# Requesting the first attention tables during the second d-projection, with four layer-norm gate tiles

## The chip, the cores and the metric

The kernel runs on one core of a Trainium2 chip. The metric is the device time of one execution in microseconds (us), taken as the median of several runs. The five engines of the core are named as in the profile: PE (matrix multiply; PEld is its weight load), DVE (vector), ACT (scalar functions), POOL (GpSimd) and SP, which here only issues DMA transfers. Each engine takes its own instructions strictly in the order in which the program lists them; engines wait for one another and for transfers through semaphores.

## The reference, cut to what matters

Two layers run over 1024 latent tokens and 256 context tokens of width 1024. The first (even) layer is attention of two kinds. The second (odd) layer is the one that the change touches: a convolution branch of 512 channels and a neighbourhood attention with eight heads of 64, whose outputs are gated and multiplied by one output matrix.

```python
def odd_mixer(...):
    cv, cgl, cg, dq, dk, dv, dg = split_cols(h_lat @ w_in, ODD_WIDTHS)
    ...
    oc = conformer_conv(cv, cgl, cg, dw_w, dw_b, ln_g, ln_b)
    ...
    def d_row(args):                       # one of 16 grid rows of 64 queries
        r, qr = args
        rs = jnp.clip(r - kh // 2, 0, rows - kh)
        ...                                # 8 rows of keys, with a column window of 16
        bias = rpb[:, dr_idx][:, :, dc_idx] + col_mask[None, None]
        ...
        return gqa_attend(qr[:, :, :, None, :], kk, vv, bias).reshape(bsz, GRID_W, D_W)
    ...
    y_lat = jnp.concatenate([oc, od * jax.nn.silu(dg)], axis=-1) @ w_out

def conformer_conv(val, glu_gate, silu_gate, dw_w, dw_b, ln_g, ln_b):
    u = val * jax.nn.sigmoid(glu_gate)
    u = lax.conv_general_dilated(u, dw_w.reshape(C_CONV, 1, C_WIDTH), ...) + dw_b
    u = jax.nn.silu(layer_norm(u, ln_g, ln_b))
    return u * jax.nn.silu(silu_gate)
```

All of it is in float32. The kernel keeps that accuracy with a high and a low part of each operand, and three matmuls where one would do (`mm3`: high by high, high by low, low by high).

## The kernel before

**How the order comes about.** The kernel is written in program order, with generators that hand the turn to one another, and a planner then lays out each engine's instructions: by priority (which is program order, moved by `later`), by what its own timeline says is ready, and by when a tile of a pool comes free. So a transfer that stands late in the program can be issued much earlier on SP, if its source is written and its tile is free. What the planner fixes is an order for each engine; at run time an engine that waits holds up all that stands behind it.

**Pools.** Tiles live in pools that are opened and closed like a stack in the on-chip memory. A tile of a pool opened later may lie where a tile of a closed pool lay; its first write then waits for the last use of the old tile.

**The stages around the change.** The odd layer runs so:

1. The pool `cv` (and `u0`, closed at `ux.close()`): the projections of the convolution branch; then `d_proj(0)`, the first of four d-projections. Beside them run the convolution's 31 taps on DVE, ACT and POOL, for four blocks of channels. Their sums go to the DRAM tensor `Uc`, and the branch's gates to `Gc`.
2. The pool `ln`: `d_proj(1)`. After each of its 31 steps `pump(1)` runs one step of `ln_steps`, the layer norm of the convolution's output, in two halves of 512 tokens (c = 0, 1).
3. The pool `d1` (`dpool`): the attention of the odd layer in 16 groups (`groups1`), each one head and one half of the grid's columns. `weave` mixes its steps with `d_proj(2)`, `d_proj(3)` and the output projection; what is woven in stands some way ahead in priority.

**A d-projection** (`d_proj(i)`) covers two heads. It loads the weights of queries and keys as eight 128 x 256 blocks (`load_w`, L329: raw tile wr in three buffers; L296 on ACT casts the high part wh, L299 on POOL subtracts the low part wl), does the queries for two chunks of 512 tokens, the keys for three chunks (the last, 256 context tokens, is the one whose operand is called hc), loads the eight blocks of values and gates, and does these. Eight buffers hold wh and wl, so a value block is cast only when the last matmul with the query and key block of the same buffer is through. Results go to the DRAM tensors `QD`, `KD`, `VD` and `GD`; the parts of queries, keys and values are called spq, spk and spv. The products go through PSUM banks of which the tag "pp" has two.

**The layer norm** (`ln_steps`): one load of 1 MB (uc, L1138), three sums on POOL (L1141 to L1143), a matmul with ones that gives the mean (mu, L1148), four subtractions (L1152) with squares, the inverse deviation (`rstd_steps`), and for each of four blocks a scaling (L1167), a tanh, an addition, a product with the tanh and a product with the gate tile gc (L1172), which has one buffer; its load (L1166) stands in the same loop, as does a store of 256 KB to `Oc` (L1173).

**The start of attention.** `attn_gen` requests the tables of the first two groups (`next(p)`, which runs `load_q`: QH twice, QL, and the bias table bm of the row maxima, 540 KB); before that, `load_head(0)` loads the head's K (KAt, two transfers of 384 KB), and `copy_k` has ACT copy half of it to KBt (L564). The first group's `start` loads the bias tables bs of groups 0 and 1 (384 KB each), the second head's K and the V tiles. `k_tiles` and `v_tiles` have POOL set the constant parts of KBt and Vt (L355, L350). All of KAt, KBt, Vt, bm and bs lie in `d1`, which is opened when `ln` is closed.

Of the kernel before, what the change touches and what calls it, by code (L numbers as in the profile page):

```python
# [10 lines left out]
F32 = mybir.dt.float32  # L11
F32R = mybir.dt.float32r
ALU = mybir.AluOpType
# [5 lines left out]
P = 128  # L19
# [46 lines left out]
SQP = ((2, 3, 4, 5, 6), (), (4, 6))  # L66
ENDS = ((0, 0, 512), (1, 0, 256), (1, 256, 256))
LATE = 100
NFILL = (34, 34, 34)
HV = (('gggvvvvg',) * 3, ('gggvvvvg', 'vvvgvvvg', 'gggvvvvg'))  # L70
O1 = (6, 84, 46, 14)
# [16 lines left out]
def tile_kernel(ctx: ExitStack, tc: tile.TileContext, a, out):  # L88
# [22 lines left out]
    def nm(s):  # L111
        uid[0] += 1
        return f"{s}_{uid[0]}"
# [286 lines left out]
    def attn_gen(pool, groups, vshare, look, nexts=None):  # L400
# [30 lines left out]
                g.finish(g.ov, rb)  # L431

        for p in preps[:2]:
            next(p)
            yield
        for _ in range(2):
            yield
# [670 lines left out]
    with ExitStack():  # L1108
# [25 lines left out]
        def ln_steps(vp, c):  # L1134

            cs = slice(c * 512, (c + 1) * 512)
            uc = vp.tile([P, 4, 512], F32, tag="uc", name=nm("uc"), bufs=2)
            SY.dma_start(uc, Uc[:, :, cs])  # L1138
            s1 = vp.tile([P, 512], F32, tag="s1", name=nm("s1"), bufs=2)
            s2 = vp.tile([P, 512], F32, tag="s2", name=nm("s2"), bufs=1)  # L1140
            GP.tensor_tensor(s1, uc[:, 0], uc[:, 1], op=ALU.add)  # L1141
            GP.tensor_tensor(s2, uc[:, 2], uc[:, 3], op=ALU.add)
            GP.tensor_tensor(s1, s1, s2, op=ALU.add)  # L1143
            yield
            for _ in range(2):
                yield
            mu = bank("st", nm("mu"))
            PE.matmul(mu, ones5, s1, start=True, stop=True)  # L1148
# [12 lines left out]
            bc = yield from rstd_steps(vp, [s1], 512, "st", 2.0)  # L1161
            SC.copy(s2, bc)
            yield
            for i in range(4):
                gc = vp.tile([P, 512], F32, tag="gc", name=nm("gc"), bufs=1)
                SY.dma_start(gc, Gc[:, i, cs])  # L1166
                VE.scalar_tensor_tensor(uc[:, i], uc[:, i], lng[:, i : i + 1], s2, op0=ALU.mult, op1=ALU.mult)  # L1167
                th = vp.tile([P, 512], F32, tag="sql", name=nm("thl"), bufs=2)
                SC.activation(th, uc[:, i], AF.Tanh, scale=0.5, bias=lnbh[:, i : i + 1])
                VE.tensor_scalar(uc[:, i], uc[:, i], lnb[:, i : i + 1], None, op0=ALU.add)  # L1170
                VE.scalar_tensor_tensor(uc[:, i], th, 1.0, uc[:, i], op0=ALU.add, op1=ALU.mult)
                VE.scalar_tensor_tensor(uc[:, i], uc[:, i], 0.25, gc, op0=ALU.mult, op1=ALU.mult)  # L1172
                SY.dma_start(Oc[:, i, cs], uc[:, i])  # L1173
                yield

        def by_col(ap, c):
            return ap.rearrange("p (t r j) -> p r t j", t=5, j=8)[:, (c - 1) * 8 : c * 8]
# [5 lines left out]
        def d_proj(i):  # L1183
# [32 lines left out]
            for c in VORD:  # L1216
                t0, n = CHUNKS[c]
                pp = yield from proj1(wh, wl, 0, c)
                if c == 0:
                    vc = half("vc", "hf")  # L1220
                    SC.copy(vc[:, :n], pp[:, :n])
                    blocks = [(j, vc[:, j * P : (j + 1) * P]) for j in range(2)]
                    yield
                else:
                    for h_ in range(2):
                        SC.copy(by_col(vT[:, h_, :], c), window(pp, h_))
                    sg = half("sgd", "hf")
                    pp = yield from proj1(wh, wl, 1, c)
                    sgh = sg.rearrange("p (h r q) -> p h r q", h=2, q=32)
                    SC.activation(sgh, halves(pp), AF.Tanh, scale=0.5)  # L1230
                    for h_ in range(2):
                        VE.scalar_tensor_tensor(sgh[:, h_], sgh[:, h_], 1.0, halves(pp)[:, h_], op0=ALU.add, op1=ALU.mult)
                    SY.dma_start(GD[i][:, :, (c - 1) * 256 : c * 256], sg.rearrange("p (h q) -> p h q", h=2))
                    blocks = [(2 + 5 * h_ + t, vT[:, h_, t * P : (t + 1) * P]) for h_ in range(2)
                              for t in range(5 * (c - 1))]
                for k0 in range(0, len(blocks), 4):
                    bl = blocks[k0 : k0 + 4]
                    tr = bank(TRV, nm("trv"))
                    for k, (_, v) in enumerate(bl):
                        PE.transpose(tr[:, k * P : (k + 1) * P], v, ident)  # L1240
                    sp = pair("spv", 640)
                    n = len(bl) * P
                    sv = sp.rearrange("p a b -> p (a b)").rearrange("p (j s d) -> p j s d", s=2, d=64)
                    src = tr[:, :n].rearrange("p (j d) -> p j d", d=64)
                    split(src, sv[:, : 2 * len(bl), 1], sv[:, : 2 * len(bl), 0], "s", "v")
                    sv = sp.rearrange("p a b -> p (a b)").rearrange("p (j e d) -> p j e d", e=2, d=P)
                    k = 0
                    while k < len(bl):
                        e = k + 1
                        while e < len(bl) and bl[e][0] == bl[e - 1][0] + 1:  # L1250
                            e += 1
                        SY.dma_start(VD[i][:, bl[k][0] : bl[k][0] + e - k], sv[:, k:e].bitcast(F32))
                        k = e

        with tc.tile_pool(name="cv", bufs=1, reuse_waits="tile") as vp:
            stg[0] = vp
# [20 lines left out]
            for _ in bg:  # L1277
                pass
        ux.close()
        with tc.tile_pool(name="ln", bufs=1, reuse_waits="tile") as vp:  # L1280
            stg[0] = vp
            lnbh = vp.tile([P, 4], F32, tag="lnbh", name="lnbh")
            VE.tensor_scalar(lnbh, lnb, 0.5, None, op0=ALU.mult)
            ones5 = vp.tile([P, P], F32, tag="ones5", name="ones5")
            VE.memset(ones5, 1.0 / 512.0)

            def lns():
                for c in range(2):
                    yield from ln_steps(vp, c)
            bg = lns()  # L1290
            for _ in d_proj(1):
                pump(1)
            for _ in bg:
                pass

        dpool = ctx.enter_context(tc.tile_pool(name="d1", bufs=1, reuse_waits="tile"))
        stg[0] = dpool
        for _ in range(2):
            k_tiles(dpool, 12, 2)
        v_tiles(dpool, 7, 2)  # L1300
        od = [None, None]

        heads = {}
# [6 lines left out]
        def group1(gi, hd, hf):  # L1310
# [4 lines left out]
            def load_q(QH, QL):  # L1315
                SY.dma_start(QH[0:64, :].bitcast(F32), QD[i][ds, 0, hf])
                SY.dma_start(QH[64:128, :].bitcast(F32), QD[i][ds, 0, hf])
                SY.dma_start(QL[0:64, :].bitcast(F32), QD[i][ds, 1, hf])
                bm = dpool.tile([P, BMW], F32, tag="bm", name=nm("bm"), bufs=2)
                SY.dma_start(bm, a["d_bm"][hd, hf])  # L1320
                for b in range(4):
                    bms[b] = bm[:, BMO[b] : BMO[b] + (KROWS[b][1] - KROWS[b][0]) * NW]
# [335 lines left out]
```

## Time and profile before

| | us |
|---|---|
| median of 3 runs | 1566.41 |
| lowest and highest run | 1565.63, 1570.52 |
| profiled execution | 1564.79 |
| its span in the profile | 1563.0 |
| busy time of PE in the span | 1445.1 |
| busy time of DVE in the span | 1123.4 |

The profile is of one execution. The span is the time from its first to its last instruction; the device time of the same execution is 1.8 us longer. "Busy" counts instructions in execution. The views used below are: the page with its totals; windows, which give busy time, the clock granted to PE (1.00 is full speed), the share of the 16 DMA engines in use and GB/s in a stretch; the chain of waits, followed back from the last instruction; the timeline of one engine, with the idle time before an instruction and what ended it in square brackets; and the list of DMA issues with the median time from issue to landing. A line number such as L1172 is one of the kernel before. An engine name with a q (SPq) marks the instruction that issues a transfer, not the transfer.

### The profile page before, as it was taken

How to read it: one execution, taken by the hardware profiler on the slowest of the kernel's cores; microseconds unless marked ns; L12 is line 12 of the kernel's file. 1: busy time of each engine (PE TensorE's matmuls, PEld its weight loads, DVE VectorE, ACT ScalarE, POOL GpSimd, SP SyncE). 2: the span in 40 equal slices, each digit the busy share in tenths (PEclk: the TensorE clock that was granted, in tenths of full speed). 3: DMA queues.
4: the chain of work that ended last, by engine and by line, in shares of the span. 5: the costliest groups of instructions: out<-in, count | busy, mean ns of one | idle time of the engine just before them, and what ended most of it. 6: DMA issues, size and time to landing. Idle time of an engine off the chain costs nothing.

```text
span 1563.0 us, 22012 instructions
## 1 busy us (share of the span) xinstructions
PE 1445.1 (92%) x6984; PEld 1173.7 (75%) x6984; DVE 1123.4 (72%) x2172; ACT 753.6 (48%) x1545; POOL 825.5 (53%) x762
## 2 busy tenths in 40 slices
PE   6989989999999999899999889999998889999894
PEld 1878868887789678678887667888776678777784
DVE  4898897689858666654677667999655467676776
ACT  2731354445454755665455646444342355555472
POOL 1462464455555676776555656655442344255564
PEclk9899989999999999999999989999999899999997
DMA  9557345423441124731111122213545767797522
GB/s 340 190 163 240 89 123 167 148 67 118 145 137 44 53 90 144 225 110 38 41 44 41 61 95 61 74 63 128 172 158 186 241 198 214 218 271 219 167 73 108
DMA packets 181259, 213.66 MB, mean 137 GB/s; under 512 B 17164, under 2 KB 134616, under 8 KB 181144
## 3 DMA queue, kind: packets, MB, share of 16 engines
q1 hardware_dynamic: 174480, 200.69, 41.3%
q10 hardware_dynamic: 6664, 11.57, 2.3%
q8 instruction: 55, 0.90, 0.2%
q14 instruction: 60, 0.49, 0.1%
HBM read 152.17 MB, written 60.03 MB: 136 GB/s over the span
## 4 chain that ended last, share of the span: by engine, by line
PE 67%; DVE 14%; DMA 11%; issue 3%; POOL 2%; ACT 2%; SPq 1%; ACTq 0%; DVEq 0%; POOLq 0%
PE p L318 7%; PE p L320 7%; PE p L319 7%; PE ov L417 4%; PE ov L419 4%; PE ov L418 4%; PE po L320 4%; PE po L319 4%; PE po L318 4%; PE st L474 4%; PE st L478 4%; DVE macc L219 3%; DMA mw<-in_mod_w_dram 3%; PE pg L319 2%; PE pg L318 2%
## 5 line engine op out<-in xcount | busy, mean ns | idle before, releaser
L299 POOL TENSOR_TENSOR pl<-pf,ph 128x512 fp32r<-128x512 f32 (+3 forms) x321 | 391.2, 1230 | 260.7 <-ACT ph L296 211.3
L299 POOL TENSOR_TENSOR wl<-wr,wh 128x256 fp32r<-128x256 f32 (+2 forms) x256 | 197.1, 786 | 223.8 <-ACT wh L296 161.4
L486 ACT ACTIVATE pf<-st 128x512 f32<-128x512 f32 x284 | 166.1, 596 | 152.8 <-PE st L478 101.4
L296 ACT CAST ph<-pf 128x512 fp32r<-128x512 f32 (+3 forms) x364 | 205.6, 579 | 22.1 <-PE ov L418 12.4
L296 ACT CAST wh<-wr 128x256 fp32r<-128x256 f32 (+2 forms) x264 | 103.3, 404 | 184.0 <-DMA wr<-in_od_d_dram 40.7
L318 PE MATMUL p<-hh,wh 128*128 128x512 f32 x448 | 177.3, 399 | 6.4 <-ACT wh L296 4.2
L319 PE MATMUL p<-hl,wh 128*128 128x512 f32 x448 | 177.1, 397 | 0.2 <-POOL hl L299 0.2
L320 PE MATMUL p<-hh,wl 128*128 128x512 f32 x448 | 175.5, 401 | 0.1
L474 PE MATMUL st<-QH,KAt 128*128 128x512 f32 (+3 forms) x364 | 142.4, 393 | 14.1 <-ACT pf L486 12.1
L417 PE MATMUL ov<-ph,Vt 128*128 128x512 f32 (+3 forms) x364 | 140.6, 386 | 8.9 <-DVE y L640 6.4
L419 PE MATMUL ov<-pl,Vt 128*128 128x512 f32 (+3 forms) x364 | 140.6, 387 | 4.0 <-DVE pl L299 2.4
L478 PE MATMUL st<-QL,KBt 68*128 68x512 f32 (+3 forms) x364 | 137.7, 387 | 0.5 <-DVE QL L388 0.3
L418 PE MATMUL ov<-ph,Vt 128*64 128x512 f32 (+3 forms) x364 | 137.7, 378 | 0.0
L1125 DVE SCALAR_TENSOR_TENSOR cps<-U,taps,cps 128x512 f32<-128x512 f32 x184 | 124.2, 749 | 0.0
L219 DVE SCALAR_TENSOR_TENSOR macc<-mw,csil,macc 128x512 f32<-128x512 f32 x107 | 99.3, 949 | 16.4 <-DMA mw<-in_mod_w_dram 15.4
L598 DVE TENSOR_REDUCE mp<-mx 128x1 f32<-128x512 f32 x128 | 85.6, 682 | 34.6 <-PE mx L597 33.8
L318 PEld LDWEIGHTS p<-hh,wh 128*128 128x128 f32 x448 | 84.8, 189 | 26.4 <-ACT wh L296 4.8
L319 PEld LDWEIGHTS p<-hl,wh 128*128 128x128 f32 x448 | 84.9, 190 | 20.2 <-POOL hl L299 0.6
L320 PEld LDWEIGHTS p<-hh,wl 128*128 128x128 f32 x448 | 84.3, 189 | 20.3 <-POOL wl L299 0.5
L474 PEld LDWEIGHTS st<-QH,KAt 128*128 128x128 f32 x364 | 70.1, 193 | 34.4 <-ACT pf L486 19.9
L419 PEld LDWEIGHTS ov<-pl,Vt 128*128 128x128 f32 x364 | 70.1, 193 | 27.9 <-POOL pl L299 5.2
L417 PEld LDWEIGHTS ov<-ph,Vt 128*128 128x128 f32 x364 | 70.3, 193 | 24.5 <-issue 7.5
(277 smaller groups left out, 3530.1 us busy)
## 6 DMA issues: line engine op xcount, KB each, us to landing
mw<-in_mod_w_dram SPq DMA_DIRECT2D x34, 512.0 KB, 5.7
Q<-qs SPq DMA_DIRECT2D x40, 256.0 KB, 2.7
QH<-Q SPq DMA_DIRECT2D x80, 128.0 KB, 2.7
bm<-in_d_bm_dram SPq DMA_DIRECT2D x16, 540.0 KB, 6.2
wr<-in_od_d_dram SPq DMA_DIRECT2D x64, 128.0 KB, 2.7
mw<-in_mod_w_dram SPq DMA_DIRECT2D x28, 256.0 KB, 3.0
wr<-in_ev_qkv_dram SPq DMA_DIRECT2D x32, 192.0 KB, 2.9
KAt<-KD SPq DMA_DIRECT2D x16, 384.0 KB, 6.8
```

The costliest lines, as they stand in the source:

```text
L219: VE.scalar_tensor_tensor(t, w, csil[:, dk, q : q + 1], t, op0=ALU.mult, op1=ALU.add)
L296: SC.copy(hi, src)
L299: (GP if leng == "g" else VE).tensor_tensor(lo, src, hi.bitcast(F32), op=ALU.subtract)
L318: PE.matmul(o, lh, rh, start=first, stop=False)
L319: PE.matmul(o, lh, rl, start=False, stop=False)
L320: done[0] = PE.matmul(o, ll, rh, start=False, stop=last)
L417: PE.matmul(o, V[:, 64:192], ph, start=(t == 0), stop=False)
L418: PE.matmul(cut(g.ov[0:64], q0, n), V[:, 0:64], ph, start=False, stop=False)
L419: pvs.append(PE.matmul(o, V[:, 64:192], pl, start=False, stop=(last and g.sink is None)))
L474: sts.append(PE.matmul(sf, KA[:, cs], cut(g.QH, q0, n), start=True, stop=False))
L478: PE.matmul(sf, KB[0:68, cs], cut(g.QL[0:68], q0, n), start=False, stop=True)
L486: SC.activation(pf[:, :n], st[:, :n], AF.Exp, scale=1.0 if g.bias else SCALE)
```

## The change

It does the following:

- Opens a pool `t1` (`tpool`) ahead of `ln`, where the conv stage's tiles lay, and puts the K tiles (KAt, KBt, with POOL's memsets), bm and bs in it. Only V and the working tiles stay in `d1`, opened after layer norm as before.
- Requests the tables of the first two groups from the loop of `d_proj(1)`: after step 2 the tables of group 0, after 4 the first head's K, after 8 its copy on ACT, after 10 the tables of group 1, after 14 and 18 the bias tables bs of the two groups. `attn_gen` then skips its own request, and the first group's `start` loads no bs.
- Gives the layer norm's gate tile four buffers and issues the four loads of a half together, three steps after its uc load and ahead of the mean.
- Replaces the four stores of a half's result by one of 1 MB, one step later.
- In `d_proj`, issues the gate store (`GD`) after the V stores (`VD`) of the same chunk.

No arithmetic is changed.

```diff
+EARLY = {2: lambda g, h, c: next(g[0].prep), 4: lambda g, h, c: h(0), 8: lambda g, h, c: c(),
+         10: lambda g, h, c: next(g[1].prep), 14: lambda g, h, c: g[0].load_bs(), 18: lambda g, h, c: g[1].load_bs()}
...
         for p in preps[:2]:
-            next(p)
+            if not layer[0]:
+                next(p)
             yield
...
             SY.dma_start(uc, Uc[:, :, cs])
+            gcs = [vp.tile([P, 512], F32, tag="gc", name=nm("gc"), bufs=4) for _ in range(4)]
...
             for _ in range(2):
                 yield
+            for i in range(4):
+                SY.dma_start(gcs[i], Gc[:, i, cs])
             mu = bank("st", nm("mu"))
...
             for i in range(4):
-                gc = vp.tile([P, 512], F32, tag="gc", name=nm("gc"), bufs=1)
-                SY.dma_start(gc, Gc[:, i, cs])
+                gc = gcs[i]
...
                 VE.scalar_tensor_tensor(uc[:, i], uc[:, i], 0.25, gc, op0=ALU.mult, op1=ALU.mult)
-                SY.dma_start(Oc[:, i, cs], uc[:, i])
                 yield
+            yield
+            SY.dma_start(Oc[:, :, cs], uc)
...
-                    SY.dma_start(GD[i][:, :, (c - 1) * 256 : c * 256], sg.rearrange("p (h q) -> p h q", h=2))
                     blocks = [(2 + 5 * h_ + t, vT[:, h_, t * P : (t + 1) * P]) for h_ in range(2)
...
+                if c:
+                    SY.dma_start(GD[i][:, :, (c - 1) * 256 : c * 256], sg.rearrange("p (h q) -> p h q", h=2))
...
         ux.close()
-        with tc.tile_pool(name="ln", bufs=1, reuse_waits="tile") as vp:
...
-        dpool = ctx.enter_context(tc.tile_pool(name="d1", bufs=1, reuse_waits="tile"))
-        stg[0] = dpool
+        tpool = ctx.enter_context(tc.tile_pool(name="t1", bufs=1, reuse_waits="tile"))
         for _ in range(2):
-            k_tiles(dpool, 12, 2)
-        v_tiles(dpool, 7, 2)
+            k_tiles(tpool, 12, 2)
...
-                bm = dpool.tile([P, BMW], F32, tag="bm", name=nm("bm"), bufs=2)
+                bm = tpool.tile([P, BMW], F32, tag="bm", name=nm("bm"), bufs=2)
...
-                bs = dpool.tile([P, BSW], F32, tag="bs", name=nm("bs"), bufs=2)
+                bs = tpool.tile([P, BSW], F32, tag="bs", name=nm("bs"), bufs=2)
...
-                for g2 in groups1[gi + 1 if gi else 0 : gi + 2]:
+                for g2 in groups1[gi + 1 : gi + 2] if gi else ():
                     g2.load_bs()
...
-        load_head(0)
-        copy_k(*heads[0])
+        with tc.tile_pool(name="ln", bufs=1, reuse_waits="tile") as vp:
...
+            for n_, _ in enumerate(d_proj(1)):
+                pump(1)
+                if n_ in EARLY:
+                    EARLY[n_](groups1, load_head, lambda: copy_k(*heads[0]))
+            for _ in bg:
+                pass
+
+        dpool = ctx.enter_context(tc.tile_pool(name="d1", bufs=1, reuse_waits="tile"))
+        stg[0] = dpool
+        v_tiles(dpool, 7, 2)
```

More of the change, by code (lines that the diff above doesn't have):

```diff
@@ L1279, in tile_kernel @@
         ux.close()
-        with tc.tile_pool(name="ln", bufs=1, reuse_waits="tile") as vp:
[L1281 to L1294, printed above, removed]
-        dpool = ctx.enter_context(tc.tile_pool(name="d1", bufs=1, reuse_waits="tile"))
-        stg[0] = dpool
+        tpool = ctx.enter_context(tc.tile_pool(name="t1", bufs=1, reuse_waits="tile"))
         for _ in range(2):
-            k_tiles(dpool, 12, 2)
-        v_tiles(dpool, 7, 2)
+            k_tiles(tpool, 12, 2)
         od = [None, None]
@@ L1401, in tile_kernel, with lns @@
         groups1 = [group1(gi, *x) for gi, x in enumerate(SEQ)]
-        load_head(0)
-        copy_k(*heads[0])
+        with tc.tile_pool(name="ln", bufs=1, reuse_waits="tile") as vp:
+            stg[0] = vp
+            lnbh = vp.tile([P, 4], F32, tag="lnbh", name="lnbh")
+            VE.tensor_scalar(lnbh, lnb, 0.5, None, op0=ALU.mult)
+            ones5 = vp.tile([P, P], F32, tag="ones5", name="ones5")
+            VE.memset(ones5, 1.0 / 512.0)
+            def lns():
+                for c in range(2):
+                    yield from ln_steps(vp, c)
+            bg = lns()
+            for n_, _ in enumerate(d_proj(1)):
[7 more added lines that the diff above has]
+        v_tiles(dpool, 7, 2)
         x2, ocs, od3, fin = [], [], [], [0]
```

## The prediction

> **What bounds the kernel now.** I read the page first, for the engine that carries the time:
>
> ```profile
> span 1563.0 us, 22012 instructions
> PE 1445.1 (92%) x6984; PEld 1173.7 (75%) x6984; DVE 1123.4 (72%) x2172; ACT 753.6 (48%) x1545; POOL 825.5 (53%) x762
> PE 67%; DVE 14%; DMA 11%; issue 3%; POOL 2%; ACT 2%; SPq 1%; ACTq 0%; DVEq 0%; POOLq 0%
> ```
>
> PE bounds the kernel: 92% busy, 67% of the chain that ended last. An edit that adds no matmul and takes none away can only change what PE loses, as idle time or at a low clock. So I asked next for windows of 10 us around the touched stage (columns: stretch, length, PE busy with its matmuls, granted clock, DMA share, GB/s):
>
> ```profile
> 1130.00:1140.00 10.00, 10.00 (x42) 1.00 0.95 325
> 1140.00:1150.00 10.00, 10.00 (x60) 1.00 0.46 174
> 1150.00:1160.00 10.00, 10.00 (x49) 1.00 0.29 89
> 1160.00:1170.00 10.00, 10.00 (x48) 1.00 0.25 81
> 1170.00:1180.00 10.00, 7.00 (x49) 1.00 0.76 265
> ...
> 1200.00:1210.00 10.00, 5.70 (x26) 0.98 0.42 136
> 1210.00:1220.00 10.00, 9.18 (x46) 0.85 1.03 309
> 1220.00:1230.00 10.00, 5.23 (x16) 0.66 1.08 324
> 1230.00:1240.00 10.00, 9.86 (x42) 0.83 0.52 174
> ```
>
> Busy time times clock is what PE did at full speed; the rest of 10 us is lost. Lost: 10 - 5.70 x 0.98 = 4.41 in 1200 to 1210, then 2.20, 6.55 and 1.82, together 14.98 us in 40 us, and 3.00 in 1170 to 1180. This is the seam between layer norm and odd attention. DMA shows the other half: full at 1130 to 1140, half empty for 30 us, full again exactly where PE starves. The chain of waits, in order of time, names the links (start, length, what):
>
> ```profile
> 1194.75 4.39 DMA gc<-Gc
> 1199.16 0.70 DVE uc L1172
> ...
> 1200.30 2.67 DMA gc<-Gc
> 1203.06 0.70 DVE uc L1172
> ...
> 1204.19 2.80 DMA gc<-Gc
> 1207.09 0.69 DVE uc L1172
> 1207.78 0.41 DVE spk L299
> ...
> 1211.48 9.92 DMA KAt<-KD
> 1221.47 8.14 DMA wr<-in_od_d_dram
> 1229.68 0.41 ACT wh L296
> 1230.14 0.79 PE p L318
> ```
>
> There are two links. First, the one gate tile: each of its loads can start only when DVE has used the one before, and DVE, which takes its work in order, keeps the key split (spk, L299) of the third d-projection behind these waits. Second, the opening burst of attention: K tables, bias tables and V go out together, the weight load wr goes out when the K table has landed, and takes 8.14 us.
>
> **The change part by part.** Gate tiles four deep. The waits it removes, and what PE pays for them, stand in the timeline:
>
> ```profile
> 1168.90 0.69 DVE L1172 SCALAR_TENSOR_TENSOR uc<-uc,gc 128x512 f32<-128x512 f32 x1 [1.22 <-DMA gc<-Gc]
> 1173.00 0.36 PE L318 MATMUL p<-hc,wh 128*128 128x256 f32 x1 [2.64 <-DVE sgd L1232]
> 1209.31 0.35 PE L318 MATMUL p<-hc,wh 128*128 128x256 f32 x1 [4.30 <-DVE spk L299]
> 1214.73 0.47 PE L1359 MATMUL mx<-KAt,QH 128*128 128x256 f32 x2 [0.82 <-DMA KAt<-KD]
> ```
>
> For the second half, three loads of 4.39, 2.67 and 2.80 us go from in front of DVE's multiplies; DVE then reaches the key split at about 1200, before PE has finished that chunk, and the 4.30 us idle at 1209.31 goes whole. What that idle left behind, the low clock in 1210 to 1220, goes with it: 2.20 less the 0.82 that waits for KAt, 1.38. Together 5.7 us. For the first half DVE gains 1.22, and the PE idle of 2.64 at 1173.00 hangs on DVE's gate multiply (L1232) behind it: 1.2 us. What is late next there is DVE's own subtraction, so I count no more.
>
> Tables early. What moves out of the burst, and the usual landing time of a weight load (KB each, median us to landing):
>
> ```profile
> bm<-in_d_bm_dram SPq DMA_DIRECT2D x16, 540.0 KB, 6.2
> wr<-in_od_d_dram SPq DMA_DIRECT2D x64, 128.0 KB, 2.7
> KAt<-KD SPq DMA_DIRECT2D x16, 384.0 KB, 6.8
> bs<-in_d_bs_dram SPq DMA_DIRECT2D x16, 384.0 KB, 4.5
> X<-x SPq DMA_DIRECT2D x4, 1024.0 KB, 4.7
> ```
>
> Two bm, two bs and the two halves of one KAt are 2 x 540 + 4 x 384 = 2616 KB, 2.68 MB; at the 309 to 324 GB/s of the burst that is 8.3 to 8.7 us of transfer. The gain lies between nothing (another wait takes over) and the 6.55 + 1.82 = 8.4 us that PE loses from 1220 to 1240. I take 8.14 - 2.7 = 5.4, what the weight load lands later than such a load usually does, because the V tables, the second head's K and the key store stay in the burst.
>
> What is added. The same 2.68 MB now share the layer-norm stretch, with two KBt memsets on POOL, the K copy on ACT and two sets of four gate loads asked for at once. The rows for it:
>
> ```profile
> 1078.54 0.48 SPq L1316 DMA_DIRECT2D QH<-QD  x1
> 1127.36 0.58 SPq L1138 DMA_DIRECT2D uc<-Uc  x1
> 1135.63 1.30 POOL L1143 TENSOR_TENSOR s<-s,s 128x512 f32<-128x512 f32 x1
> 1137.98 1.02 PE L1148 MATMUL mu<-s,ones 128*128 128x512 f32 x2
> 1209.99 2.69 POOL L355 MEMSET KBt<- 4x1536 f32 x2 [23.65 <-DMA Oc<-uc]
> 1212.98 1.47 ACT L564 CAST KBt<-KAt 64x1536 fp32r<-64x1536 f32 x1 [3.94 <-DMA KAt<-KD]
> 1221.48 1.47 ACT L564 CAST KBt<-KAt 64x1536 fp32r<-64x1536 f32 x1 [5.85 <-DMA KAt<-KD]
> ```
>
> The program asks for QH after layer norm, yet it goes out at 1078.54: the planner sends what is ready and has a tile. So I expect the early tables at about 1127, when the conv tiles are free, and not spread over steps 2 to 18; the second head's K, whose tile now lies in the early pool too, may follow. The room is there: 325 GB/s less 174, 89 and 81 leaves 6.3 MB in 1140 to 1170. The order is the risk: ACT waited 3.94 and 5.85 us in front of its two K copies, with everything behind them, since the plan thought the table landed sooner. The cost here lies between nothing and 8.3 us, the whole transfer put in front of the weights of the second d-projection. I take 2.0, half of the nearest row (3.94), for PE has a second PSUM bank to go on with while ACT stands. The memsets (2.69 us) run where POOL is idle, or cost up to that ahead of a weight split; this is inside the bounds.
>
> The rest. The skipped request in the attention loop and the skipped bias load of the first group are these same DMAs, counted above. Eight output stores become two of 1 MB: six issues fewer on SP, and the last store starts at about 1201 instead of 1207.8. A 1 MB store took 4.7 us (X<-x), so the V memset that must wait for it comes at about 1206, not later than POOL's memset now (1209.99). The gate store of the second chunk goes behind three VD stores; the gates are read a group later, so nothing. No wait is added on PE; on ACT the K copy moves ahead of layer-norm squares and weight casts, on POOL the memsets move ahead of weight splits.
>
> Sum against the profiled execution, which took 1564.79 us (span 1563.0 and 1.8 around it): -5.7 - 1.2 - 5.4 + 2.0 = **-10.3 us**, 1554.5. The median of the runs shown, 1566.41, lies 1.6 higher; against it I forecast 1556.1. A measurement of this kernel can tell about 0.3%, 4.7 us, from no change.
>
> **The rivals.** *The burst was covered anyway.* The v weights can be cast only when PE is through with the key chunk that frees their buffers, and V, the second K and the key store stay. For it: the weight load waits for a KAt landing, and one of them stays. Then only the gate terms count: -5.7 - 1.2 + 2.0 = -4.9, 1561.5. Tables that come no earlier than now, because their space is not free, give the same; against that, the conv stage is over at 1127.
>
> *The wait moves to ACT.* Two K copies stand in front of casts and squares in the layer-norm stretch, each waiting as now, 3.94 + 5.85 = 9.8 us, with no cover: -12.3 + 9.8 = -2.5, 1563.9. Against it: the stretch has free DMA, and chunks of PE work to hide a few us.
>
> *Slower: the tables stand in front of layer norm on SP's queue.* All the tables and the four gate loads (1 MB more) go out ahead of uc at 1127 and of the wr behind. 3.7 MB at 325 GB/s is 11.4 us; the sum for mu has 1.05 us to spare (POOL ends at 1136.93, PE takes mu at 1137.98), so PE stands 10.3 us, loses 1.4 more at low clock as after the 4.30 idle, and the layer-norm chain ends as late as before, so the gate terms go. What is left is 11.7 - 5.4 = +6.3, 1572.7. It decides once the delay passes about 10 us. Against it: uc is asked for earlier in the program than the tables. [...]
>
> **How the numbers follow.** Forecast (about -7 to -18) 0.60; burst covered 0.13; ACT 0.17; slower 0.10. Faster by over 0.3% is the first two, 0.73; within 0.3% 0.17; slower 0.10. The low end takes the whole 14.98 and the first 3.00 back at no cost, -18.0: 1548. The high end takes in the burst and ACT rivals, 1567; left out are the slower case and a tail of ACT's, under 0.2.
>
> **What would show it.** Right: no wait of L1172 on gc; no PE idle over 1 us behind spk; bm, bs and KAt landed before 1180; the first wr of the burst landing in under 4 us; DMA share above 0.5 in 1140 to 1160; PE at clock 1.00 through the seam. Wrong: ACT waiting for KAt, or mu's matmul waiting for POOL, in 1127 to 1160; PE below 10.00 in 1130 to 1170; or the loss in 1200 to 1240 staying above 8 us.

## The result and the profile after

| | before | after |
|---|---|---|
| median of 4 runs, us | 1566.11 | 1540.06 |
| lowest and highest run | 1565.63, 1570.52 | 1537.48, 1543.79 |
| profiled execution | 1564.79 | 1537.48 |

The kernel is 26.05 us faster; the ratio is 0.983, 95% interval 0.980 to 0.986. The forecast was 1556.1 and its range 1548 to 1567: the direction was right, the gain two and a half times what was forecast, and the time lies below the range. Among the runs of all kernels in this document one, of e3 below, was slow at 4820.52 us, three times the others of its kernel; it stands in no figure here.

The page of the kernel after, in the same three lines (span; busy time of the engines; shares of the chain that ended last):

```profile
span 1535.7 us, 21991 instructions
PE 1437.1 (94%) x6984; PEld 1165.5 (76%) x6984; DVE 1115.5 (73%) x2172; ACT 753.6 (49%) x1545; POOL 821.0 (53%) x762
PE 17%; DMA 4%; DVE 3%; issue 1%; ACT 1%; POOL 1%; SPq 0%; DVEq 0%; POOLq 0%; ACTq 0%
```

The shares of the chain add up to 27%: here it could be followed back only to 1119.63, so this line says nothing beside that of before. The other two do: the same 6984 matmuls, in a span 27.3 us shorter, so what went is time that PE lost. To see where, I cut both runs at the same four pieces of work: the first gate chunk of the second d-projection (vc, L1221 before, L1227 after), the last query split of the third (spq, L1190 and L1196), the gating of the second group's output (y, L1388 and L1377), that of the last group, and the last step of the output. The stretches are called layer norm, seam, attention and tail below. Windows of the kernel before (stretch, length, PE busy with its matmuls, granted clock, DMA share, GB/s):

```profile
1117.92:1190.30 72.38, 68.92 (x338) 1.00 0.57 195
1190.30:1276.86 86.56, 70.34 (x328) 0.88 0.68 205
1276.86:1528.25 251.39, 239.16 (x1210) 0.98 0.66 192
1528.25:1559.66 31.41, 15.00 (x76) 0.70 0.31 112
```

and of the kernel after:

```profile
1120.04:1194.52 74.48, 70.67 (x342) 0.98 0.76 250
1194.52:1250.44 55.92, 54.65 (x274) 1.00 0.70 207
1250.44:1503.60 253.16, 245.71 (x1262) 0.99 0.66 197
1503.60:1531.52 27.92, 15.75 (x76) 0.68 0.32 117
```

Length less busy time times clock is what PE lost (the clock is rounded, so about 1 us is open in each long stretch):

| lost by PE, us | layer norm | seam | attention | tail |
|---|---|---|---|---|
| before | 3.5 | 24.7 | 17.0 | 20.9 |
| after | 5.2 | 1.3 | 9.9 | 17.2 |
| difference | +1.7 | -23.4 | -7.1 | -3.7 |

The differences add up to 32.5 us where the four stretches together are 30.3 us shorter; the rest is that rounding. The layer-norm stretch pays for the early tables, and on balance about what was forecast (2.0), though not where it was forecast, as shown further down. All the rest is more gain than forecast, and most of it is in the seam, where next to nothing is lost now. The windows of 10 us of the kernel after, with the same columns, answer to those of the prediction:

```profile
1140.00:1150.00 10.00, 9.45 (x56) 1.00 1.04 321
1150.00:1160.00 10.00, 8.31 (x34) 0.83 0.94 329
1160.00:1170.00 10.00, 10.00 (x45) 1.00 0.16 48
...
1200.00:1210.00 10.00, 9.12 (x40) 1.00 0.43 140
1210.00:1220.00 10.00, 9.69 (x59) 1.00 1.00 321
1220.00:1230.00 10.00, 9.93 (x51) 1.00 0.79 237
1230.00:1240.00 10.00, 10.00 (x52) 1.00 0.50 138
```

From 1200 to 1240 PE loses 0.88 + 0.31 + 0.07 = 1.26 us where it lost 14.98, with the DMA engines just as full at 1210 to 1220. And the loss went beyond that stretch. Two idle times of PE in the kernel before lie on either side of the prediction's window (timeline of PE; in brackets the idle time before the instruction and what ended it):

```profile
1192.03 0.47 PE L318 MATMUL p<-hh,wh 128*128 128x512 f32 x1 [2.19 <-DVE spq L1192]
1269.96 0.47 PE L1359 MATMUL mx<-KAt,QH 128*128 128x256 f32 x2 [3.87 <-DMA QH<-QD]
```

The kernel after has neither; these are its idle times between 1120 and 1270:

```profile
1151.69 0.80 PE L322 MATMUL p<-hh,wl 128*128 128x512 f32 x1 [2.25 <-POOL wl L301]
1177.87 0.36 PE L320 MATMUL p<-hc,wh 128*128 128x256 f32 x1 [1.57 <-ACT spv L298]
1207.56 1.01 PE L1356 MATMUL mx<-KAt,QH 128*128 128x440 f32 x2 [0.42 <-DVE mp L1359]
1210.10 0.62 PE L481 MATMUL st<-QL,KBt 68*128 68x512 f32 x2 [0.30 <-DVE QL L390]
1260.29 0.48 PE L1348 MATMUL mx<-KAt,QH 128*128 128x256 f32 x2 [0.45 <-DMA QH<-QD]
```

What PE does in the seam instead shows in the view of the tile mx, the row maxima of the scores (duration in ns, first and last start, forms), and in the timeline of ACT at the first exponential of attention (pf). Before, the two views one after the other:

```profile
L1370 DVE CUSTOM_DVE_ANT_0 mx<-mx,bm x22: 481/600/625, 1216.2 to 1295.6; 128x440 f32<-128x440 f32 x12, 128x320 f32<-128x320 f32 x10
```

```profile
1229.99 0.59 ACT L486 ACTIVATE pf<-st 128x512 f32<-128x512 f32 x1
```

After:

```profile
L1359 DVE CUSTOM_DVE_ANT_0 mx<-mx,bm x28: 485/564/654, 1195.5 to 1295.8; 128x440 f32<-128x440 f32 x14, 128x320 f32<-128x320 f32 x14
```

```profile
1210.63 0.60 ACT L489 ACTIVATE pf<-st 128x512 f32<-128x512 f32 x1 [3.41 <-PE st L481]
```

The maxima of the first groups start 20.7 us earlier (1216.2 to 1195.5), between the matmuls of the third d-projection, and the first exponential 19.4 us earlier. In the kernel before, PE did the last of the first maxima, from 1220.00 on, with no projection beside them, and then stood until the value weights of that projection were cast (timeline of PE):

```profile
1230.14 0.79 PE L318 MATMUL p<-hh,wh 128*128 128x512 f32 x1 [3.83 <-ACT wh L296]
```

This is the theory that I took into the experiments, called **theory L**: with K and the bias tables in place, the maxima and K copies of the first groups are done beside the third d-projection, attention starts earlier and stays ahead of what is woven into it, so that waits behind the seam go too. Against it stand **the recorded sum** (the gain is the bytes that leave the burst and the gate waits), and **rival G** (attention waits for the end of the layer norm, so the gate tiles make it).

### The profile page after: what moved, and what is told of

Same layout as the page of the kernel before. It is cut to its first block, busy times and chain, and to the rows that moved or that the text cites. A ratio compares the mean times of both kernels' runs of the same rounds, so it can differ in the third digit from the quotient of the medians.

```text
span 1535.7 us, 21991 instructions
## 1 busy us (share of the span) xinstructions
PE 1437.1 (94%) x6984; PEld 1165.5 (76%) x6984; DVE 1115.5 (73%) x2172; ACT 753.6 (49%) x1545; POOL 821.0 (53%) x762
## 5 line engine op out<-in xcount | busy, mean ns | idle before, releaser
L301 POOL TENSOR_TENSOR wl<-wr,wh 128x256 fp32r<-128x256 f32 (+2 forms) x256 | 193.1, 770 | 215.1 <-ACT wh L298 162.1
L477 PE MATMUL st<-QH,KAt 128*128 128x512 f32 (+3 forms) x364 | 141.0, 389 | 16.8 <-ACT pf L489 16.3
```

The lines of the kernel that those rows point to most:

```text
L301: (GP if leng == "g" else VE).tensor_tensor(lo, src, hi.bitcast(F32), op=ALU.subtract)
L477: sts.append(PE.matmul(sf, KA[:, cs], cut(g.QH, q0, n), start=True, stop=False))
```

## The experiments

The kernel before took 1565.0 to 1565.5 us beside every one of them; single runs lie up to 7.5 us from the median of their kernel (3 to 12 runs each), so I read nothing into a difference of less than 4 us between medians. Each kernel has one profile, of one run.

**The two halves of the change alone.** First the gate tiles and the merged store in the kernel before (e1), then the tables alone, with the layer norm as before (e2):

```diff
+            gcs = [vp.tile([P, 512], F32, tag="gc", name=nm("gc"), bufs=4) for _ in range(4)]
...
+            for i in range(4):
+                SY.dma_start(gcs[i], Gc[:, i, cs])
...
-                gc = vp.tile([P, 512], F32, tag="gc", name=nm("gc"), bufs=1)
-                SY.dma_start(gc, Gc[:, i, cs])
+                gc = gcs[i]
...
-                SY.dma_start(Oc[:, i, cs], uc[:, i])
                 yield
+            yield
+            SY.dma_start(Oc[:, :, cs], uc)
```

> The kernel before with the four gate tiles and the merged stores alone; K, bm and bs stay in the late pool. By the recorded sum: 5.7 + 1.2 = 6.9 us faster than before, about 1559. Theory L (the tables' early landing carries the change: the first two groups' row maxima and both K copies are done beside the third d-projection, attention starts earlier and leads the projections woven in, so that later waits go too): 3 to 8 us faster, with the burst of tables and a PE loss of 6 us or more still there after the layer norm. Rival G (the end of the layer norm is what attention waits for, since its tiles free V and the working tiles): 18 to 26 us faster, nearly the whole.

> The changed kernel with one gate tile, loaded in the loop, and a store for each block. By the recorded sum: 5.4 - 2.0 = 3.4 us faster than before, about 1563. Theory L: 14 to 22 us faster than before (1544 to 1552), group 0 of attention done more than 10 us earlier than in the kernel before. Rival G: 0 to 6 us faster.

Measured: gates alone 1551.08 (ratio 0.993, 0.990 to 0.995), 13.9 us off; tables alone 1547.18 (0.987, 0.983 to 0.991), 17.8 us off. By the recorded terms it would have been 6.9 and 3.4. Both halves are undersized, and they overlap: 13.9 + 17.8 is 5.6 more than the 26.05 of the two together. Of the forecasts, theory L's was right for the tables (14 to 22) and wrong for the gates (3 to 8). Rival G's was wrong for both (18 to 26 for the gates, 0 to 6 for the tables), and it falls as the whole story.

Why the gates do more than their own waits shows in the timeline of SP. The kernel before, and then the kernel with the gates alone, at the first load of K:

```profile
1208.23 1.14 SPq L361 DMA_DIRECT2D KAt<-KD  x2
```

```profile
1199.34 1.97 SPq L361 DMA_DIRECT2D KAt<-KD  x2
```

The pool `d1` has its place only when the layer norm's tiles are done with, so a layer norm that ends earlier sends the whole burst 8.9 us earlier, and the first exponential comes 10.9 us earlier, at 1219.09. The term of the first half, on the other hand, wasn't there: the idle of 2.64 us before the gate multiply of the second d-projection stands unchanged with the gates alone:

```profile
1173.94 0.36 PE L318 MATMUL p<-hc,wh 128*128 128x256 f32 x1 [2.65 <-DVE sgd L1235]
```

**Place or request.** The early pool stays, but the tables are asked for where they were before (e3):

```diff
         for p in preps[:2]:
-            if not layer[0]:
-                next(p)
+            next(p)
...
-                for g2 in groups1[gi + 1 : gi + 2] if gi else ():
+                for g2 in groups1[gi + 1 if gi else 0 : gi + 2]:
...
-                if n_ in EARLY:
-                    EARLY[n_](groups1, load_head, lambda: copy_k(*heads[0]))
...
+        load_head(0)
+        copy_k(*heads[0])
```

> The changed kernel with the early pool, but all requests at their old places in the program, after the layer norm. If the place in memory decides, since the planner sends what is ready and has a tile: within 4 us of the changed kernel (1540), the tables still landing before 1160, behind the second uc load. If the requests in the loop decide: 1550 or more, tables landing after 1190.

Measured: 1543.43 (0.985, 0.981 to 0.990), 21.6 us off and within the 4 us of the kernel after that was expected if the place decides; the tables of the first two groups go out between 1128 and 1139, and the maxima start at 1189.0. The place alone does most of it: with a tile free and the source written, the planner sends the tables early wherever the program asks. Its layer-norm stretch differs most from that of the kernel after:

```profile
1114.70:1196.21 81.51, 73.19 (x347) 0.96 0.71 225
```

Here PE loses 81.51 - 73.19 x 0.96 = 11.2 us against 5.2. I read this as a better order that the spread requests set among work that goes out early in either case; as the medians are only 3.4 us apart, it isn't shown that it pays.

**Which table counts.** In each of these one table goes back into the late pool with its old request: the bias tables of the maxima (e5), the other bias tables (e6), both heads' K (e7), the second head's K alone (e4).

```diff
...
-                bm = tpool.tile([P, BMW], F32, tag="bm", name=nm("bm"), bufs=2)
+                bm = dpool.tile([P, BMW], F32, tag="bm", name=nm("bm"), bufs=2)
```

```diff
...
-                bs = tpool.tile([P, BSW], F32, tag="bs", name=nm("bs"), bufs=2)
+                bs = dpool.tile([P, BSW], F32, tag="bs", name=nm("bs"), bufs=2)
```

```diff
...
-        for _ in range(2):
-            k_tiles(tpool, 12, 2)
...
         dpool = ctx.enter_context(tc.tile_pool(name="d1", bufs=1, reuse_waits="tile"))
+        for _ in range(2):
+            k_tiles(dpool, 12, 2)
+        load_head(0)
+        copy_k(*heads[0])
```

```diff
-        for _ in range(2):
-            k_tiles(tpool, 12, 2)
+        k_tiles(tpool, 12, 1)
...
+        k_tiles(dpool, 12, 1)
```

> The changed kernel with the bias table of the row maxima (bm) back in the late pool: the first two groups' maxima cannot be taken before the layer norm is over, K and bs still land early; 1.08 MB more in the opening burst. If the maxima taken early are what the seam gains (theory L): 4 to 9 us slower than the changed kernel, with the maxima's matmuls and their DVE reductions in one row behind the layer norm. If only the bytes in the burst count: 1.1 MB at 320 GB/s, 3.4 us slower at most. If only K's landing counts: within 2 us.

> The changed kernel with the bias tables of the score tiles (bs) back in the late pool, 0.79 MB more in the burst. They are wanted only at the second tile of group 0, after its maxima. Theory L: within 3 us of the changed kernel. Bytes alone: 2.5 us slower. If every table counts alike: 5 us or more slower.

> The changed kernel with both K tiles back in the late pool, bm and bs still early; 1.57 MB more in the burst, and the two K copies on ACT at its start again. Nothing of attention can start before K: theory L: 8 to 14 us slower than the changed kernel (1548 to 1554), near the kernel with the gate tiles alone (1551). Bytes alone: 4.9 us slower.

> The changed kernel with only the second head's K tile back in the late pool, so its load and its copy on ACT cannot come before the end of the layer norm. If the ACT wait of 5.68 us in front of the second copy costs what PE loses from 1140 to 1160 (3.85 us) and the seam does not need that K early: 2 to 4 us faster than the changed kernel, 1536 to 1538. If the second K in the opening burst is what held attention back in the kernel before (9.92 us landing): 4 to 10 us slower than the changed kernel, 1544 to 1550.

| late | median | ratio (95%) | first maximum with bm | median less that of after |
|---|---|---|---|---|
| bm | 1555.84 | 0.994 (0.991 to 0.996) | 1213.5 | +15.8 |
| both heads' K | 1549.86 | 0.991 (0.988 to 0.993) | 1211.9 | +9.8 |
| bs | 1546.96 | 0.989 (0.986 to 0.991) | 1183.4 | +6.9 |
| second head's K | 1541.84 | 0.985 (0.982 to 0.989) | 1193.9 | +1.8 |

The maxima need K and bm; without either of them they are late, and 9.8 or 15.8 us of the gain are gone, though the other tables lie ready. The bytes alone would have cost 3.4 us at most for bm and 4.9 for both K, by the expectations. bm, 1080 KB, costs more late than the two heads' K, 1536 KB, though of the 6.0 us between the two kernels about 4 lie in the layer-norm stretch (9.4 us lost with bm late, 5.3 with K late). Theory L had 4 to 9 for bm, which was too little, and 8 to 14 for both K. For the second head's K alone neither forecast came: 2 to 4 faster or 4 to 10 slower was expected, and 1.8 slower isn't told from nothing. In both kernels without early maxima the seam is partly back, here with bm late (its seam, then its idle time at the third group's queries):

```profile
1196.43:1274.28 77.85, 69.47 (x342) 0.93 0.62 198
```

```profile
1260.97 0.77 PE L1347 MATMUL mx<-KAt,QH 128*128 128x256 f32 x2 [3.94 <-DMA QH<-QD]
```

and here with K late:

```profile
1193.70:1265.95 72.25, 63.94 (x318) 0.95 0.69 204
```

```profile
1260.22 0.47 PE L1346 MATMUL mx<-KAt,QH 128*128 128x256 f32 x2 [3.16 <-DMA QH<-QD]
```

PE loses 77.85 - 69.47 x 0.93 = 13.2 and 11.5 us there, and the wait for QH behind 1260 returns with them. The bias tables bs aren't needed for the maxima, and theory L expected at most 3 us for them; 6.9 were measured, which was the sign that every table counts alike. But the maxima stay early there, and what late bs costs lies in the layer-norm stretch (8.8 us lost, by the same working, against 5.2). With bs late POOL waits 11.32 us for the second uc, where it waits 3.40 in the kernel after, and PE waits for the weight split that stands behind this on POOL (timeline of PE with bs late):

```profile
1148.22 0.80 PE L322 MATMUL p<-hh,wl 128*128 128x512 f32 x1 [4.23 <-POOL wl L301]
```

That load takes about 13 us in both kernels, from its issue to the sum that waits for it; what differs is that with bs late three weight splits stand behind that sum on POOL, and after the change two. Why they stand so I don't know, beyond the new order.

**The test of theory L.** All tables of the first two groups early, as in the kernel after; only the first twelve steps of attention, which are the maxima of the first two groups and what belongs to them, are held until the keys of the third d-projection are done (e11):

```diff
-        weave(main, WV[0], d_proj(2), 31, False, True, LAG[0])
+        ahead2 = d_proj(2)
+        for _ in range(15):
+            with later(FL[1]):
+                next(ahead2)
+        for _ in range(12):
+            with tc.issue_after(done[0].ins):
+                next(main)
+        weave(main, WV[0] - 12, ahead2, 16, False, True, LAG[0])
```

> The kernel after, with every transfer of the tables as early as there, but the matmuls of the first two groups' row maxima held until the keys of the third d-projection are done, which is where they stood before the change. Theory L (the gain in the seam is the maxima done beside the third d-projection): most of it goes though the tables are in place, 8 to 15 us slower than the kernel after, 1548 to 1556, near the kernels with bm late or K late, with over 5 us of PE loss back in the seam. The theory of the recorded sum (the transfers leave the burst): within 3 us of the kernel after, since no byte moves back. If it comes out near the kernel after, theory L falls.

Measured: 1556.9 (0.995, 0.994 to 0.997), 16.8 us slower than the kernel after, just past the upper end that theory L gave and far from the other theory's 3. The tables go out as early here, in the timeline of SP:

```profile
1126.78 0.61 SPq L1309 DMA_DIRECT2D bm<-in_d_bm_dram  x1
1130.10 1.24 SPq L363 DMA_DIRECT2D KAt<-KD  x2
```

The view of mx and the timeline of ACT of the same kernel:

```profile
L1359 DVE CUSTOM_DVE_ANT_0 mx<-mx,bm x23: 489/615/657, 1212.1 to 1299.5; 128x440 f32<-128x440 f32 x12, 128x320 f32<-128x320 f32 x11
```

```profile
1230.11 0.60 ACT L489 ACTIVATE pf<-st 128x512 f32<-128x512 f32 x1 [5.59 <-PE st L481]
```

With bm and K asked for between 1126 and 1132, the first exponential stands at 1230.11 again, where it stood before the change (1229.99). Its windows by stretch:

```profile
1117.38:1191.49 74.11, 70.55 (x340) 0.98 0.75 249
1191.49:1278.18 86.69, 80.46 (x392) 0.96 0.58 181
1278.18:1520.67 242.49, 227.56 (x1146) 0.98 0.66 189
1520.67:1548.61 27.94, 16.04 (x76) 0.64 0.32 117
```

Lost: 5.0, 9.5, 19.5 and 17.7 us. Against the kernel after that is 8.2 more in the seam and 9.6 more in the attention behind it, with the layer-norm stretch unchanged. So most of the gain goes with the early start of attention, though the tables are in place and the weight load of the burst is out even earlier, at 1208.06.

Four things limit this reading. Held like this, the kernel is still 8.5 us faster than the kernel before, with attention starting at the same time; that is near the 10.3 us of the recorded sum, though that it is the same waits and bytes isn't shown. The hold also takes back what the gates alone gave: with no table early, they had the first exponential at 1219.09, and that kernel is 5.8 us faster than this one. So 16.8 us is the early start that both halves bring; what the tables add to the gates is 1551.08 - 1540.06 = 11.0. And the maxima don't stand alone here as they did before the change: from 1210.54 to 1230 they run between the matmuls of the third d-projection without a wait of PE, and the loss lies before and after them, more than half of it in the attention behind the seam. How the late start turns into lost time is therefore not shown. The hold also changes the order that the planner finds for the rest; the size is that of one such plan.

**The gate burst and the small edits.** Two gate tiles in the loop (e10); and one tile for the first half with four for the second, asked for behind the value weights (e12), meant to be faster than the kernel after:

```diff
-            gcs = [vp.tile([P, 512], F32, tag="gc", name=nm("gc"), bufs=4) for _ in range(4)]
...
-                gc = gcs[i]
+                gc = vp.tile([P, 512], F32, tag="gc", name=nm("gc"), bufs=2)
+                SY.dma_start(gc, Gc[:, i, cs])
```

```diff
...
-            for i in range(4):
-                SY.dma_start(gcs[i], Gc[:, i, cs])
+            if c:
+                with tc.issue_after(raws[-1].ins):
+                    for i in range(4):
+                        SY.dma_start(gcs[i], Gc[:, i, cs])
...
-                gc = gcs[i]
+                if c:
+                    gc = gcs[i]
+                else:
+                    gc = vp.tile([P, 512], F32, tag="gc0", name=nm("gc"), bufs=1)
+                    SY.dma_start(gc, Gc[:, i, cs])
```

> The changed kernel with two gate tiles instead of four, loaded in the loop. If the fourfold request costs what PE loses in 1140 to 1160 (1 MB in front of the weights of the second d-projection; with one gate tile that stretch loses 2 us less) and two tiles are enough to keep DVE from waiting: 1 to 3 us faster than the changed kernel. If DVE still waits on the gates at the end of the layer norm: 2 to 5 us slower.

> The kernel after, but the first half of the layer norm has one gate tile loaded in its loop as before, and the second half has four, asked for only behind the value weights of the second d-projection, so that the eight gate loads leave the full stretch of the transfers. If the 5.4 us that PE loses in the layer-norm stretch come from the four gate loads at its start, 1 to 4 us faster than the kernel after, 1535 to 1539, with the loss of the stretch near 2.6 as with one gate tile. If they come from the tables, or the order of ACT's copies, no change, within 2 us. If the waits of the first half's one tile come back as in the kernel before (1.2 us there), up to 2 us slower.

Measured: 1547.91 (0.989, 0.986 to 0.992) and 1545.19 (0.987, 0.985 to 0.989), 7.9 and 5.1 us slower than the kernel after, and both slower than any forecast. Two tiles in the loop lost 7.1 us in the layer-norm stretch and 16.9 in attention, against 5.2 and 9.9, while the seam stayed at 5.7; whether depth or the other order does that, this run can't part. The idea behind the second fell: its layer-norm stretch lost 6.6 us, not the 2.6 of the tables alone. With one tile the loads of the first half's gates came late, DVE waited up to 2.26 us for one of them, and PE stood behind DVE again (timelines of SP and of PE):

```profile
1168.11 3.96 SPq L1177 DMA_DIRECT2D gc<-Gc  x2
```

```profile
1179.19 0.41 PE L1251 MATMUL trv<-ident,vc 128*128 128x128 f32 x2 [3.55 <-DVE spv L301]
```

Last, the two edits that the prediction put at nothing, undone one at a time in the kernel after: the gate store ahead of the V stores (e8), and a store for each block of the layer norm (e9).

```diff
+                    SY.dma_start(GD[i][:, :, (c - 1) * 256 : c * 256], sg.rearrange("p (h q) -> p h q", h=2))
                     blocks = [(2 + 5 * h_ + t, vT[:, h_, t * P : (t + 1) * P]) for h_ in range(2)
...
-                if c:
-                    SY.dma_start(GD[i][:, :, (c - 1) * 256 : c * 256], sg.rearrange("p (h q) -> p h q", h=2))
```

```diff
+                SY.dma_start(Oc[:, i, cs], uc[:, i])
                 yield
-            yield
-            SY.dma_start(Oc[:, :, cs], uc)
```

> The kernel after with the gate store ahead of the stores of V, as in the kernel before. All theories: nothing, within 3 us of the kernel after. A loss of more than that would show that the order of these stores sets a wait.

> The kernel after with four stores of 256 KB per half of the layer norm in place of one of 1 MB. The recorded prediction counts the merged store at nothing: within 3 us of the kernel after. A gain would show that the late last store, behind which the memset of the V tile waits 8.66 us on POOL in the kernel after, costs something; a loss, that the eight issues on SP do.

Measured: 1538.92 (0.983, 0.980 to 0.985) and 1542.36 (0.985, 0.983 to 0.988), both within 3 us of the kernel after: nothing that these runs can tell, as predicted.

**All kernels in one row.** The start of the first maximum with bm (the row shown above, read in every kernel) parts them into two groups:

| first maximum | kernels and their medians |
|---|---|
| 1178 to 1196 | after 1540.1; e8 1538.9; e4 1541.8; e9 1542.4; e3 1543.4; e12 1545.2; e6 1547.0; e2 1547.2; e10 1547.9 |
| 1210 to 1217 | e7 1549.9; e1 1551.1; e5 1555.8; e11 1556.9; before 1565.5 |

Every kernel of the first group is faster than every one of the second. Inside a group this start says nothing, and the edge between them is only 2 us wide: other losses of some us move each kernel too. The first exponential, read in the timeline of ACT in every kernel, says more. It stands at 1205.5 to 1213.9 in the first group; in the second it stands at 1219.1 (e1), 1222.5 (e7), 1226.2 (e5), 1230.1 (e11) and 1230.0 (before), and their medians rise in this order but for 1.2 us between e1 and e7. That e11 and before start alike and are 8.5 us apart shows again that the start isn't the whole.

## Why the prediction was right and wrong

**Gate tiles, second half.** Right in mechanism: no wait of the gate product on gc is left, and no PE idle over 1 us behind spk. Too small: I priced the idle it removes (5.7), not that the end of the layer norm also frees the place of `d1`, which sends the burst 8.9 us earlier.

**Gate tiles, first half** (1.2). Not there: the wait of 1.22 us on gc goes, but with the gates alone PE stands 2.65 us at the same place. In the kernel after that idle is gone, and PE stands 1.57 us behind ACT a little later; with the tables alone 0.90 us are left of it. So there it hung on the order of other work, not on the gate tiles.

**The added cost** (2.0). The size, 1.7 us net, was right by luck; the place was wrong. The term was half of ACT's wait in front of a K copy. Two of the prediction's signs of being wrong came: ACT waited for KAt, and PE was below 10.00 between 1140 and 1160. But the wait that PE pays for is another: the second uc, issued at 1136.74 behind tables, kept POOL waiting for 3.40 us, and a weight split behind that on POOL kept PE for 2.25 (timelines of SP, ACT and POOL of the kernel after):

```profile
1132.34 1.18 SPq L363 DMA_DIRECT2D KAt<-KD  x2
1136.74 0.58 SPq L1141 DMA_DIRECT2D uc<-Uc  x1
1138.58 2.15 SPq L363 DMA_DIRECT2D KAt<-KD  x2
```

```profile
1140.29 1.47 ACT L567 CAST KBt<-KAt 64x1536 fp32r<-64x1536 f32 x1 [2.62 <-DMA KAt<-KD]
1152.97 1.47 ACT L567 CAST KBt<-KAt 64x1536 fp32r<-64x1536 f32 x1 [5.68 <-DMA KAt<-KD]
```

```profile
1149.70 1.26 POOL L1145 TENSOR_TENSOR s<-uc 128x512 f32<-128x512 f32 x1 [3.40 <-DMA uc<-Uc]
1150.91 1.41 POOL L301 TENSOR_TENSOR wl<-wr,wh 128x256 fp32r<-128x256 f32 x2
```

No wait of PE between 1120 and 1170 stands behind the 8.3 us of ACT, so the rival in which the wait moves to ACT priced a wait that PE had work to cover. PE's idle of 2.25 us at 1151.69, shown above, ends with the split of 1150.91, and the low clock behind it costs 1.4 more (8.31 x 0.17). That is the slower rival in small, behind the second uc and not the first: 3.7 us. Whether that load took about 13 us for its place behind the tables, as the rival's sum assumes, or for the full DMA engines (a share of 1.04 from 1140 to 1150), no run here shows. With the 1.57 behind ACT these 3.7 make up the 5.2 us of the stretch; that the kernel before lost 3.5 there, by the idle of 2.64 for the most part, brings the net to 1.7. The moved requests did leave the idle stretch partly unused: 1160 to 1170 still has a DMA share of 0.16.

**Tables early: the step that failed.** "I take 5.4, what the weight load lands later than such a load usually does." It bounded the gain by the bytes that leave the burst and sized it by one landing. The first weight load of the burst did come down, to 4.18 us (the chain of waits of the kernel after; I had said under 4):

```profile
1216.39 4.18 DMA wr<-in_od_d_dram
```

But that isn't where most of the gain is. With K and bm in place, PE and DVE do the first maxima between the matmuls of the third d-projection, and attention starts 19.4 us earlier. Held back to the old start with the tables as early, the kernel loses 16.8 us. The tables were priced at 5.4 - 2.0 = 3.4 net; they bring 17.8 us alone and 11.0 on top of the gates. The prediction counted the transfers that move and the wait behind them, and put the computation that was waiting for them at nothing, without a reason.

**The edge of the sum: the second failure.** The sum ended at 1240 and took the rest as fixed. The seam reaches from the idle of 2.19 at 1192 to that of 3.87 at 1270, 24.7 us in all, and the attention behind it lost 7.1 us less. Holding the maxima brings 8.2 us of loss back in the seam and 9.6 in the attention behind it, where even more is lost then than before the change (19.5 against 17.0). So both belong to the start of attention, at least in part; that it works through attention's lead on the projections woven in is argued, not shown.

**What stays open.** The tail, 31.4 us before and 27.9 after, is 27.9 also with the gates alone and with the maxima held, and 31.4 with the second K late: it hangs on the planner's order and not on the maxima, and I didn't find on what.

## What to carry to other kernels

When operands come earlier, ask first which work was waiting for them, and what starts earlier with it; here the bytes and the landing of a transfer, priced at 5.4 us, were the smaller part of the 11.0 to 17.8 us that the tables brought. Then follow the sum to the point where both kernels do the same work again, not to the end of the stretch that caught the eye. Under this planner, which sends what has a free tile, the place of a tile decided when it was loaded, and the end of the pool that lies there is part of the price.

## What was not expected of the hardware

The granted clock fell after idle times of PE of only about 2 us: in the kernel after, the idle of 2.25 us at 1151.69 is followed by 0.83 in 1150 to 1160. In windows of 1 us the clock there is 0.72, 0.50, 0.50 and 0.57 from 1151 to 1155 and 1.00 around them, that is 3.4 us at half speed. With the maxima held it fell after an idle of 1.88 us, to 0.83 in its window of 10 us (timeline of PE and a window):

```profile
1251.83 0.73 PE L1356 MATMUL mx<-KAt,QH 128*128 128x440 f32 x1 [1.88 <-DVE mp L1350]
```

```profile
1250.00:1260.00 10.00, 8.17 (x33) 0.83 0.72 248
```

Yet the idle of 2.64 us at 1173.00 in the kernel before left the clock at 1.00 in its window of 10 us, and in each window of 1 us from 1170 to 1180. Why the clock stayed there after the longer idle no run here shows.

A DMA share of 0.76 over the layer-norm stretch, against 0.57 before, and 1.04 in its fullest 10 us, came with only 1.7 us more lost by PE in that stretch.
